# Weights' columns dealt by turns in SBUF, and activations at eight places: one step of a two-layer decoder on Trainium2

## The chip, the cores and the metric

The kernel runs on one core of one Trainium2 chip. The time is device microseconds of one execution. The kernel before took 2747.49 us in the median of three runs (2746.3 to 2748.06). A separate execution was profiled.

The core's engines work from queues of their own: TensorE (matmuls, in the profile PE, and its weight loads, PEld), ScalarE (ACT), VectorE (DVE), GpSimd (POOL) and SyncE (SP, which only issues transfers here).

## The reference

One inference step over 320 tokens, of which 256 are a prompt and 64 are 8 samples of 8 new tokens, with a model width of 2048. Layer 0 mixes tokens by gated linear attention with a carried state, layer 1 by a spatial gate over chunks of 128 positions. Each is followed by a squared-ReLU MLP of width 8192 and each sublayer by a layer norm on the scaled residual:

```python
def sq_relu_mlp(x, w1, w2):
    return jnp.square(jax.nn.relu(x @ w1)) @ w2
...
proj = x @ w_in                                  # gla: q, k, v, r, low-rank gate
...
z = jax.nn.gelu(x @ w_in + b_in, approximate=False)   # spatial gate
...
x = layer_norm(DEEPNORM_ALPHA * x + h, ln1_g[i], ln1_b[i])
x = layer_norm(DEEPNORM_ALPHA * x + sq_relu_mlp(x, mlp_w1[i], mlp_w2[i]), ln2_g[i], ln2_b[i])
```

All inputs are float32. Outputs are the 320 rows, the final states of the attention layer, and the normalised rows of the spatial gate for the samples.

## The kernel before

Activations lie transposed: 128 features on the partitions, 16 k tiles, 320 tokens along the free dimension, so a k tile is 1280 bytes of each partition. Every large product is made of units of weights: 4 k tiles by 256 output features. `unit` (L117) loads one such block of 512 KB with SyncE into `raw` (three buffers), ScalarE casts it to the rounded format `fp32r` as `wh` (L128), and VectorE forms the rest, `wl` = `raw` - `wh` (L129). Activations are split in the same way into a high and a low part, named by the stage: `xh`/`xl` (the layer's input), `oh`/`ol` (attention's output), `yh`/`yl` (the normed input of an MLP or of the spatial gate), `hh`/`hl` (the MLP's inner activations), `ph`/`pl` (the gate's output), `dgh`/`dgl` (a norm's raw input).

`mm3` (L136) issues three matmuls into one PSUM bank for a k tile and one of the two feature tiles `n` of a unit:

```python
nc.tensor.matmul(ps, wl[:, kk, s], x_h, start=first, stop=False)   # L139
nc.tensor.matmul(ps, wh[:, kk, s], x_l, start=False, stop=False)   # L140
nc.tensor.matmul(ps, wh[:, kk, s], x_h, start=False, stop=last)    # L141
```

The stationary operand is 128 x 128 words of weights, the moving operand 128 x 320 words of activations. Each matmul has a weight load of its own. A unit is 2 x 4 x 3 = 24 matmuls, and `group` (L143) runs over four units in the k direction for one or two blocks of 256 columns before the PSUM banks are evicted.

The buffers of `wh` and `wl` are a ring: four of each in ring `a`. When the attention stage is nearly over, its buffers are released (`second_half`, L612) and a second ring `b` of four and four is opened; from then on units take the rings by turns. `bigtile` (L170 and after) allots the activations' tiles with 322 words per k tile; the argument `starts` shifts a view by some words inside its tile. The MLP (L784) runs in four chunks of 2048 inner features: a product with `w1` to `hh`/`hl`, then a product with `w2` that is added to the residual `z`.

The order on each engine is set by the framework's scheduler from the program's dependencies and its own costs; semaphores between engines follow from the tiles. In the attention stage the steps of the recurrence (class `Head`) are laid between units as side work. Three of its tiles matter here: `kend` and `vfm`, which share one tag with two buffers, and the square `sq` in `sample_o` (L571), which has a buffer of its own.

Of the kernel before, what the change touches and what calls it, by code (L numbers as in the profile page):

```python
# [8 lines left out]
F32 = mybir.dt.float32  # L9
F32R = mybir.dt.float32r  # L10
# [5 lines left out]
P = 128  # L16
D = 2048
KT = D // P
TP = 256
DB, DS = 8, 8  # L20
T = TP + DB * DS
TW = T + 2
# [8 lines left out]
UK = 4  # L31
UN = 256
NU = KT // UK


V_BG, V_NG = 0, 8
# [5 lines left out]
class Ring:  # L42


    def __init__(self, pool, tag):
        self.pool, self.tag = pool, tag


class Side:
# [17 lines left out]
def step_kernel(ctx: ExitStack, tc: tile.TileContext, A):  # L67
    nc = tc.nc
    uid = [0]

    def nm(s):
        uid[0] += 1
        return f"{s}_{uid[0]}"


    cp = ctx.enter_context(tc.tile_pool(name="cp", bufs=1))
    big = ctx.enter_context(tc.tile_pool(name="big", bufs=1))
    wraw = ctx.enter_context(tc.tile_pool(name="wraw", bufs=3))
    wa = ctx.enter_context(tc.tile_pool(name="wa", bufs=4))
# [2 lines left out]
    gl = gls.enter_context(tc.tile_pool(name="gl", bufs=4, space=bass.MemoryType.PSUM))  # L82
    mx = None

    rings = [Ring(wa, "a")]
    turn = [0]
    banks = [0]
    units = [0]
# [20 lines left out]
    nc.vector.memset(eps_l[:], LN_EPS)  # L109
    eps_h = cp.tile([P, 1], F32, tag="epsh", name="eps_h")  # L110
    nc.vector.memset(eps_h[:], HEAD_EPS)

    def col(c):
        return vec[:, c : c + 1]


    def unit(w, row0, q, col0, ring):  # L117

        raw = wraw.tile([P, UK, UN], F32, tag="raw", name=nm("raw"))
        src = w[row0 // (UK * P) + q, col0 // UN]  # L120
        hi = ring.pool.tile([P, UK, UN], F32R, tag="h" + ring.tag, name=nm("wh"))
        lo = ring.pool.tile([P, UK, UN], F32R, tag="l" + ring.tag, name=nm("wl"))
        units[0] += 1
        step = 2 if units[0] <= 2 else UK
        for k in range(0, UK, step):
            ks = slice(k, k + step)
            nc.sync.dma_start(raw[:, ks, :], src[:, ks, :])
            nc.scalar.copy(hi[:, ks, :], raw[:, ks, :])  # L128
            nc.vector.tensor_sub(lo[:, ks, :], raw[:, ks, :], hi[:, ks, :].bitcast(F32))  # L129
        return hi, lo  # L130

    def next_ring():
        turn[0] += 1
        return rings[turn[0] % len(rings)]

    def mm3(ps, wh, wl, kk, n, rh, rl, k, c0, cn, first, last):  # L136
        s = slice(n * P, (n + 1) * P)
        x_h, x_l = rh[:, k, c0 : c0 + cn], rl[:, k, c0 : c0 + cn]
        nc.tensor.matmul(ps, wl[:, kk, s], x_h, start=first, stop=False)  # L139
        nc.tensor.matmul(ps, wh[:, kk, s], x_l, start=False, stop=False)  # L140
        nc.tensor.matmul(ps, wh[:, kk, s], x_h, start=False, stop=last)  # L141

    def group(w, row0, cols, rh, rl, evict, side=None, width=T, before=None):  # L143

# [25 lines left out]
    lp = l2 = z = None  # L170
# [4 lines left out]

    def bigtile(tag, dt, name, width=T, start=0):

        t = (lp if tag == "b1" else big).tile([P, KT * TW], dt, tag=tag, name=nm(name))
        return t[:, start : start + KT * width].rearrange("p (k t) -> p k t", t=width)

    def parts(pair, name, width=T, starts=(0, 0)):
        return (bigtile(pair + "0", F32R, name + "h", width, starts[0]),
                bigtile(pair + "1", F32R, name + "l", width, starts[1]))
# [5 lines left out]
    gp = gst.enter_context(tc.tile_pool(name="gp", bufs=1))  # L189
    g2 = gst.enter_context(tc.tile_pool(name="g2", bufs=2))  # L190
# [28 lines left out]
    for c in range(2):  # L219
        m = gp.tile([P, 4, DS], F32, tag=f"ms{c}", name=f"ms{c}")  # L220
# [72 lines left out]
    class Head:  # L293


        def __init__(hd, h):
            hd.h = h
            hd.eb, hd.ei, hd.ee = {}, {}, {}
# [261 lines left out]
        def sample_o(hd):  # L560
            h, s1 = hd.h, hd.s1
            os_ = gp.tile([P, DV], F32, tag="sq", name=nm("os"))
            nc.scalar.copy(os_[:], hd.po[:])
            pt = gltile()
            for vt in range(4):
                nc.tensor.transpose(pt[:, vt * P : (vt + 1) * P], os_[:, vt * P : (vt + 1) * P], ident[:])
            pv = pt[:].rearrange("p (v c t) -> p v c t", v=4, c=2)
            o_s = o_all[:, 4 * h : 4 * h + 4, TP:T]
            nc.scalar.copy(o_s, pv[:, :, 0, :])
            nc.vector.tensor_add(o_s, o_s, pv[:, :, 1, :])  # L570
            sq = gp.tile([P, 4, DB * DS], F32, tag="sqs", name=nm("sq"))  # L571
            nc.scalar.activation(sq[:], o_s, AF.Square)
            nc.vector.tensor_reduce(s1[:, TP:T], sq[:].rearrange("p v t -> p t v"), axis=AX.X, op=ALU.add)

            pr = gltile(T)
            nc.tensor.matmul(pr[:], ones[:], s1[:], start=True, stop=True)
            hd.rs = gp.tile([P, T], F32, tag="rs", name=nm("rs"))
            rsqrt(hd.rs[:], pr[:], 1.0 / DV, HEAD_EPS, eps_h, gp)
# [17 lines left out]
    for h, hd in enumerate(hds):  # L596
        gates = [hd.gate_logits, hd.gate_sums, hd.gate_decays]
        first = [lambda: [load_x(1), load_gates()], lambda: [load_x(q) for q in (2, 3)], low_gate, *gates]
# [13 lines left out]
    def second_half():  # L612

        nonlocal lp, l2, z, gl, mx
        side.flush()
        split_o(range(4 * (H - 1), 4 * H))
        gst.close()
        gls.close()
        gl = ctx.enter_context(tc.tile_pool(name="gs", bufs=2, space=bass.MemoryType.PSUM))
        mx = ctx.enter_context(tc.tile_pool(name="mx", bufs=2, space=bass.MemoryType.PSUM))  # L620
        banks[0] = 3
        lp = ctx.enter_context(tc.tile_pool(name="lp", bufs=1))
        l2 = ctx.enter_context(tc.tile_pool(name="l2", bufs=2))
        wb = ctx.enter_context(tc.tile_pool(name="wb", bufs=4))
        rings.append(Ring(wb, "b"))
        z = lp.tile([P, KT, T], F32, tag="z", name="z")
        for q in range(2):
            nc.gpsimd.dma_start(z[:, 8 * q : 8 * q + 8, :], xT[:, 8 * q : 8 * q + 8, :])
# [122 lines left out]
    def gemm_of(norm, out, w, col0, evict_raw, evict, starts=(0, 0)):  # L751

        yh, yl = parts(out, "y", starts=starts)
        norm.close()
        side = Side([lambda j=j: norm.apply(j, yh, yl) for j in range(KT)], 3 * NU)
        group(w, 0, (col0, col0 + UN), *norm.raw, evict_raw, side, width=TW)
        side.flush()
        for i in range(2, D // UN):
            group(w, 0, (col0 + i * UN,), yh, yl, lambda n, ps, i=i: evict(2 * i + n, ps))
        return yh, yl  # L760
# [23 lines left out]
    def mlp(i, norm, y_in, h_in, vg, vb, raw, last=False):  # L784

        w1, w2 = A["mlp_w1"][i], A["mlp_w2"][i]
        NC_ = 4
        for c in range(NC_):
            hs = []

            def sq_relu(j, x, r):
                if not hs:
                    hs.extend(parts(h_in, "h", starts=(8 * c, 8 * c) if i == 0 else (0, 8 * c)))
                hh, hl = hs
                f = l2.tile([P, T], F32, tag="f", name=nm("f"))
                nc.vector.scalar_tensor_tensor(f[:], x, 0.0, r[:], op0=ALU.max, op1=ALU.mult)
                nc.scalar.copy(hh[:, j, 0:T], f[:])
                nc.vector.tensor_sub(hl[:, j, 0:T], f[:], hh[:, j, 0:T].bitcast(F32))

            def evict(j, ps):  # L800
                r = l2.tile([P, T], F32, tag="r", name=nm("r"))
                nc.scalar.activation(r[:], ps[:], AF.Relu)  # L802
                sq_relu(j, ps[:], r)

            def evict_raw(j, ps):
                t, wb_ = norm.correct(ps)
                r = l2.tile([P, T], F32, tag="r", name=nm("r"))
                nc.scalar.activation(r[:], t[:], AF.Relu, bias=wb_)
                sq_relu(j, r[:], r)

            if c == 0:
                yh, yl = gemm_of(norm, y_in, w1, 0, evict_raw, evict, starts=(0, 0) if i == 0 else (32, 0))
            else:
                gemm(w1, 0, c * D, yh, yl, evict)
            if c < NC_ - 1:
                def evz(j, ps, s=ALPHA if c == 0 else 1.0):
                    nc.vector.scalar_tensor_tensor(z[:, j, :], z[:, j, :], s, ps[:], op0=ALU.mult, op1=ALU.add)
                gemm(w2, c * D, 0, *hs, evz)
            else:
                return residual_gemm(w2, *hs, c * D, 1.0, vg, vb, raw, last=last)  # L820
# [4 lines left out]
    def before(q):  # L825
        if q == NU - 1:
            second_half()

    norm = residual_gemm(A["gla_w_out"], oh, ol, 0, ALPHA, V_L1G, V_L1B, "b", quad=True,
                         side=side, before=before)  # L830
    norm = mlp(0, norm, "a", "b", V_L2G, V_L2B, "a")


# [40 lines left out]
    yh, yl = gemm_of(norm, "b", A["sg_w_in"], D, ev_v_raw, lambda j, ps: put_v(j, ps[:], col(V_SB + KT + j)))  # L874
# [49 lines left out]

    norm = residual_gemm(A["sg_w_out"], ph, pl, 0, ALPHA, V_L1G + KT, V_L1B + KT, "a", quad=True)
    norm = mlp(1, norm, "b", "a", V_L2G + KT, V_L2B + KT, "b", last=True)


    on_pool = (5, 9, 13)
    dh, dl = norm.raw  # L930
    ps = {}
# [98 lines left out]
```

## Time and profile before

| | |
|---|---|
| median of three runs | 2747.49 us |
| the profiled execution | 2747.28 us |
| its span, first to last instruction | 2745.6 us |
| TensorE busy | 2726.5 us in 18,493 matmuls |
| VectorE busy | 1544.6 us |
| ScalarE busy | 1182.2 us |
| mean granted clock of TensorE | 0.999 |
| transfers | 434.51 MB, mean 158 GB/s |

In the profile a line such as L141 is a line of the kernel. A group's row has line, engine, operation, output <- inputs, partitions x elements and count, then busy microseconds and mean nanoseconds of one, then the engine's idle time ahead of these instructions and what ended it. Matmuls are pipelined, so their durations overlap; the distance from start to start tells what one costs. In a view by windows, each engine has its busy time and its number of instructions, and behind them stand the granted clock, the share of the DMA engines and GB/s. A waits row reads: who <- for whom, microseconds in total, times, the longest.

### The profile page before, as it was taken

How to read it: one execution, taken by the hardware profiler on the slowest of the kernel's cores; microseconds unless marked ns; L12 is line 12 of the kernel's file. 1: busy time of each engine (PE TensorE's matmuls, PEld its weight loads, DVE VectorE, ACT ScalarE, POOL GpSimd, SP SyncE). 2: the span in 40 equal slices, each digit the busy share in tenths (PEclk: the TensorE clock that was granted, in tenths of full speed). 3: DMA queues.
4: the chain of work that ended last, by engine and by line, in shares of the span. 5: the costliest groups of instructions: out<-in, count | busy, mean ns of one | idle time of the engine just before them, and what ended most of it. 6: DMA issues, size and time to landing. Idle time of an engine off the chain costs nothing.

```text
span 2745.6 us, 44621 instructions
## 1 busy us (share of the span) xinstructions
PE 2726.5 (99%) x18493; PEld 2703.0 (98%) x18493; DVE 1544.6 (56%) x2284; ACT 1182.2 (43%) x1698; POOL 54.4 (2%) x84
## 2 busy tenths in 40 slices
PE   8999999999999999999999999999999999999998
PEld 8999999999999999999999999999999999999998
DVE  6577577885444434444468774686444444444446
ACT  5545455464334334323345554455334333323433
POOL 1000000000000000000001000000000000000001
PEclk9999999999999999999999999999999999999999
DMA  6557566644444444444445444454444444444442
GB/s 224 178 191 237 163 209 212 208 145 154 152 148 153 147 150 150 152 148 150 150 146 169 148 138 130 141 160 154 147 153 147 153 149 151 149 151 149 151 148 75
DMA packets 126395, 434.51 MB, mean 158 GB/s; under 512 B 13680, under 2 KB 17904, under 8 KB 126192
## 3 DMA queue, kind: packets, MB, share of 16 engines
q1 hardware_dynamic: 118800, 407.29, 47.4%
q0 software_dynamic: 6512, 23.20, 2.4%
q8 instruction: 144, 2.36, 0.4%
q10 hardware_dynamic: 880, 1.18, 0.1%
q14 instruction: 59, 0.48, 0.1%
HBM read 409.60 MB, written 22.02 MB: 157 GB/s over the span
## 4 chain that ended last, share of the span: by engine, by line
PE 98%; DVE 1%; ACT 1%; DMA 0%; issue 0%; SPq 0%; ACTq 0%; DVEq 0%
PE mm L139 31%; PE mm L141 31%; PE mm L140 31%; PE gl L551 1%; PE gl L554 1%; PE gl L509 1%; DMA xr<-xT 0%; PE gl L889 0%; PE gl L493 0%; ACT z L963 0%; PE gl L884 0%; PE gl L494 0%; PE gl L418 0%; PE gl L420 0%; PE gl L472 0%
## 5 line engine op out<-in xcount | busy, mean ns | idle before, releaser
L129 DVE TENSOR_TENSOR wl<-raw,wh 128x1024 fp32r<-128x1024 f32 (+1 forms) x738 | 900.9, 1222 | 966.2 <-ACT wh L128 963.7
L128 ACT CAST wh<-raw 128x1024 fp32r<-128x1024 f32 (+1 forms) x738 | 771.0, 1046 | 1235.4 <-PE mm L141 1120.1
L141 PE MATMUL mm<-yh,wh 128*128 128x320 f32 x2368 | 730.9, 309 | 0.0
L140 PE MATMUL mm<-yl,wh 128*128 128x320 f32 x2368 | 728.5, 308 | 0.0
L139 PE MATMUL mm<-yh,wl 128*128 128x320 f32 x2368 | 725.5, 309 | 0.0
L141 PE MATMUL mm<-hh,wh 128*128 128x320 f32 x2048 | 632.2, 309 | 0.0
L139 PE MATMUL mm<-hh,wl 128*128 128x320 f32 x2048 | 631.8, 309 | 0.0
L140 PE MATMUL mm<-hl,wh 128*128 128x320 f32 x2048 | 631.4, 308 | 0.0
L140 PEld LDWEIGHTS mm<-yl,wh 128*128 128x128 f32 x2368 | 444.8, 188 | 0.0
L141 PEld LDWEIGHTS mm<-yh,wh 128*128 128x128 f32 x2368 | 444.0, 188 | 0.0
L139 PEld LDWEIGHTS mm<-yh,wl 128*128 128x128 f32 x2368 | 443.0, 188 | 0.0
L139 PEld LDWEIGHTS mm<-hh,wl 128*128 128x128 f32 x2048 | 385.0, 188 | 0.0
L140 PEld LDWEIGHTS mm<-hl,wh 128*128 128x128 f32 x2048 | 384.5, 188 | 0.0
L141 PEld LDWEIGHTS mm<-hh,wh 128*128 128x128 f32 x2048 | 384.3, 188 | 0.0
L139 PE MATMUL mm<-xh,wl 128*128 128x320 f32 x768 | 242.1, 316 | 8.7 <-ACT xh L202 5.6
L140 PE MATMUL mm<-xl,wh 128*128 128x320 f32 x768 | 240.8, 314 | 0.0
L141 PE MATMUL mm<-xh,wh 128*128 128x320 f32 x768 | 239.2, 311 | 0.0
L139 PEld LDWEIGHTS mm<-xh,wl 128*128 128x128 f32 x768 | 145.8, 190 | 13.6 <-ACT xh L202 5.6
L140 PEld LDWEIGHTS mm<-xl,wh 128*128 128x128 f32 x768 | 145.8, 190 | 3.5 <-issue 1.2
L141 PEld LDWEIGHTS mm<-xh,wh 128*128 128x128 f32 x768 | 145.9, 190 | 1.3
L139 PE MATMUL mm<-ph,wl 128*128 128x320 f32 x256 | 78.6, 309 | 1.0 <-ACT ph L922 1.0
L802 ACT ACTIVATE r<-mm 128x320 f32<-128x320 f32 x120 | 52.5, 438 | 62.1 <-PE mm L141 62.1
(271 smaller groups left out, 2490.2 us busy)
## 6 DMA issues: line engine op xcount, KB each, us to landing
raw<-mlp_w SPq DMA_DIRECT2D x512, 512.0 KB, 3.5
raw<-gla_w_in SPq DMA_DIRECT2D x94, 512.0 KB, 3.8
raw<-sg_w_in SPq DMA_DIRECT2D x64, 512.0 KB, 3.6
st<-state SPq DMA_DIRECT2D x32, 512.0 KB, 4.2
o_state_s<-st POOLq DMA_DIRECT2D x32, 512.0 KB, 4.1
raw<-gla_w_out SPq DMA_DIRECT2D x32, 512.0 KB, 3.7
raw<-sg_w_out SPq DMA_DIRECT2D x32, 512.0 KB, 3.6
z<-xT POOLq DMA_DIRECT2D x2, 1280.0 KB, 11.3
```

The lines of the kernel that those rows point to most:

```text
L128: nc.scalar.copy(hi[:, ks, :], raw[:, ks, :])
L129: nc.vector.tensor_sub(lo[:, ks, :], raw[:, ks, :], hi[:, ks, :].bitcast(F32))
L139: nc.tensor.matmul(ps, wl[:, kk, s], x_h, start=first, stop=False)
L140: nc.tensor.matmul(ps, wh[:, kk, s], x_l, start=False, stop=False)
L141: nc.tensor.matmul(ps, wh[:, kk, s], x_h, start=False, stop=last)
L509: nc.tensor.matmul(pu[:], hd.ktp[:, blk, kt * P : (kt + 1) * P], hd.vtp[:, blk, :], start=(blk == 0), stop=(blk == 1))
L551: nc.tensor.matmul(po[:], qm[:, kt, b * P : (b + 1) * P], part[:], start=False, stop=(b == DB - 1 and kt == 1 and part is sth))
L554: nc.tensor.matmul(pu[:], kz[:, g, i, kt * P : (kt + 1) * P], hd.vts[:, g, :], start=True, stop=True)
L802: nc.scalar.activation(r[:], ps[:], AF.Relu)
```

## The change

The words of a unit's weights are laid out in another order in SBUF. In ring `a` (`k` = 1) the columns of the two feature tiles take turns: word 2c is column c of the first, word 2c + 1 column c of the second. In ring `b` (`k` = 2) the two feature tiles of two k tiles take turns, four columns in 16 bytes. So a weight load reads 128 words with a step of 8 bytes in ring `a` and of 16 bytes in ring `b`, where it read 512 contiguous bytes. The cast and the subtraction write in that step; `raw` is read as before.

Second, all tiles of activations and weights are set to start at a multiple of 256 bytes or of 128 bytes (small filling tiles see to it; `wl` lies 128 bytes off `wh`). Third, the views of the MLP's activations start at places that differ from chunk to chunk, given by a table: eight places, 32 bytes apart within 256 bytes, one for each of the four chunks in the two layers, where the high and the low part come to lie at the same place. Fourth, `sq` in `sample_o` takes a buffer of the tag that `kend` and `vfm` have.

```diff
+LINE = 64
+BIG = KT * T + LINE
+
+PLACES = [[(0, 32), (16, 48), (32, 0), (48, 16), (0, 32)],
+          [(8, 8), (24, 24), (40, 40), (56, 56), (16, 32)]]
...
-    def __init__(self, pool, tag):
-        self.pool, self.tag = pool, tag
+    def __init__(self, pool, tag, k):
+        self.pool, self.tag, self.k, self.gap = pool, tag, k, False
+
+    def part(self, p, name):
+
+        t = self.pool.tile([P, UK, UN], F32R, tag=p + self.tag, name=name)
+        if not self.gap:
+            self.pool.tile([P, LINE // 2], F32, tag="gap", name=name + "_gap", bufs=1)
+            self.gap = True
+        return t[:].rearrange("p k n -> p (k n)").rearrange("p (a c m) -> p a m c", c=P, m=2 * self.k)
...
-    rings = [Ring(wa, "a")]
+    rings = [Ring(wa, "a", 1)]
...
-        hi = ring.pool.tile([P, UK, UN], F32R, tag="h" + ring.tag, name=nm("wh"))
-        lo = ring.pool.tile([P, UK, UN], F32R, tag="l" + ring.tag, name=nm("wl"))
+        hi = ring.part("h", nm("wh"))
+        lo = ring.part("l", nm("wl"))
...
-            nc.scalar.copy(hi[:, ks, :], raw[:, ks, :])
-            nc.vector.tensor_sub(lo[:, ks, :], raw[:, ks, :], hi[:, ks, :].bitcast(F32))
-        return hi, lo
+            a = slice(k // ring.k, (k + step) // ring.k)
+            r = raw[:, ks, :].rearrange("p (a k) (n c) -> p a (k n) c", k=ring.k, c=P)
+            nc.scalar.copy(hi[:, a], r)
+            nc.vector.tensor_sub(lo[:, a], r, hi[:, a].bitcast(F32))
+        return [lambda kk, n, t=t: t[:, kk // ring.k, 2 * (kk % ring.k) + n] for t in (hi, lo)]
...
-        s = slice(n * P, (n + 1) * P)
         x_h, x_l = rh[:, k, c0 : c0 + cn], rl[:, k, c0 : c0 + cn]
-        nc.tensor.matmul(ps, wl[:, kk, s], x_h, start=first, stop=False)
-        nc.tensor.matmul(ps, wh[:, kk, s], x_l, start=False, stop=False)
-        nc.tensor.matmul(ps, wh[:, kk, s], x_h, start=False, stop=last)
+        nc.tensor.matmul(ps, wl(kk, n), x_h, start=first, stop=False)
+        nc.tensor.matmul(ps, wh(kk, n), x_l, start=False, stop=False)
+        nc.tensor.matmul(ps, wh(kk, n), x_h, start=False, stop=last)
...
-        t = (lp if tag == "b1" else big).tile([P, KT * TW], dt, tag=tag, name=nm(name))
+        t = (lp if tag == "b1" else big).tile([P, BIG], dt, tag=tag, name=nm(name))
...
-            sq = gp.tile([P, 4, DB * DS], F32, tag="sqs", name=nm("sq"))
+            sq = g2.tile([P, 4, DB * DS], F32, tag="vfm", name=nm("sq"))
...
-        rings.append(Ring(wb, "b"))
+        rings.append(Ring(wb, "b", 2))
+        wb.tile([P, 3 * LINE // 4], F32, tag="fill", name="fill_b", bufs=1)
...
-                    hs.extend(parts(h_in, "h", starts=(8 * c, 8 * c) if i == 0 else (0, 8 * c)))
+                    hs.extend(parts(h_in, "h", starts=PLACES[i][c]))
...
-                yh, yl = gemm_of(norm, y_in, w1, 0, evict_raw, evict, starts=(0, 0) if i == 0 else (32, 0))
+                yh, yl = gemm_of(norm, y_in, w1, 0, evict_raw, evict, starts=PLACES[i][-1])
```

The order of instructions stays the same on SyncE and GpSimd, and almost the same on the other engines. In the second half ScalarE's row keeps its order and the casts change their form. The place is the first MLP's norm, where casts stand between the parts of `y`; first the kernel before, then the changed one (a number behind a name is a buffer's).

```order
L729 ACTIVATE z<-t_6066,vec 128x320
L728 ACTIVATE yh_6011<-t_6102,vec 128x320
L729 ACTIVATE z<-t_6102,vec 128x320
L128 CAST wh_6549<-raw_6548 128x1024
L728 ACTIVATE yh_6011<-t_6108,vec 128x320
L729 ACTIVATE z<-t_6108,vec 128x320
L128 CAST wh_6579<-raw_6578 128x1024
```

```order
L745 ACTIVATE z<-t_6070,vec 128x320
L744 ACTIVATE yh_6015<-t_6106,vec 128x320
L745 ACTIVATE z<-t_6106,vec 128x320
L144 CAST wh_6553<-raw_6552 128x2x4x128
L744 ACTIVATE yh_6015<-t_6112,vec 128x320
L745 ACTIVATE z<-t_6112,vec 128x320
L144 CAST wh_6583<-raw_6582 128x4x2x128
```

Ring `b` has the form 2x4x128 (two groups of four columns by turns) and ring `a` 4x2x128; nothing is moved there.

What does move lies in the attention stage, where the square's new buffer sets a new order on VectorE. It is the place where the second head's keys are evicted and the first head is finished, before and after.

```order
L372 TENSOR_TENSOR kend_1675<-kte_1667,fac 128x256
L378 TENSOR_TENSOR kst_1677<-kte_1667,kst_1677 128x8x16
L364 TENSOR_TENSOR kte_1667<-mm_1277,ee_1333 128x320
L570 TENSOR_TENSOR o_all_90<-o_all_90,gl_1576 128x4x64
L365 TENSOR_TENSOR kip_1666<-mm_1277,ei_1318 128x256
L366 TENSOR_TENSOR kis_1668<-mm_1277,ei_1318 128x256
L129 TENSOR_TENSOR wl_1782<-raw_1780,wh_1781 128x1024
L372 TENSOR_TENSOR kend_1693<-kte_1667,fac 128x256
L378 TENSOR_TENSOR kst_1695<-kte_1667,kst_1695 128x8x16
L397 SCALAR_TENSOR_TENSOR qd_1664<-mm_1278,eb_1311 128x320
L573 TENSOR_REDUCE s_132_1012<-sq_1583 128x64
```

```order
L387 TENSOR_TENSOR kend_1677<-kte_1669,fac 128x256
L393 TENSOR_TENSOR kst_1697<-kte_1669,kst_1697 128x8x16
L412 SCALAR_TENSOR_TENSOR qd_1666<-mm_1280,eb_1313 128x320
L588 TENSOR_REDUCE s_132_1014<-sq_1585 128x64
L472 SCALAR_TENSOR_TENSOR o_all_91<-o_all_91,vec,sr_1075 128x320
L472 SCALAR_TENSOR_TENSOR o_all_91<-o_all_91,vec,sr_1077 128x320
L472 SCALAR_TENSOR_TENSOR o_all_91<-o_all_91,vec,sr_1274 128x320
L472 SCALAR_TENSOR_TENSOR o_all_91<-o_all_91,vec,sr_1276 128x320
L412 SCALAR_TENSOR_TENSOR qd_1666<-mm_1281,eb_1319 128x320
L415 TENSOR_TENSOR qx_1667<-qd_1666,fac 128x192
L415 TENSOR_TENSOR qx_1667<-qd_1666,fac 128x128
L387 TENSOR_TENSOR kend_1695<-kte_1669,fac 128x256
```

The first `kend` has moved down to where the second stood, and the second goes behind the reduction of the square, whose buffer it waits for. On TensorE the transposes of `kend` follow, at the same place:

```order
L140 MATMUL mm_1718<-xl_89,wh_1751 128x320
L141 MATMUL mm_1718<-xh_88,wh_1751 128x320
L576 MATMUL gl_1586<-s_132_1012,ones 128x320
L382 MATMUL gl_1680<-ident,kend_1675 128x128 x2
L384 MATMUL gl_1680<-ident,kst_1677 128x128 x2
L382 MATMUL gl_1698<-ident,kend_1693 128x128 x2
L384 MATMUL gl_1698<-ident,kst_1695 128x128 x2
L139 MATMUL mm_1718<-xh_88,wl_1752 128x320
```

```order
L155 MATMUL mm_1720<-xl_90,wh_1753 128x320
L156 MATMUL mm_1720<-xh_89,wh_1753 128x320
L591 MATMUL gl_1588<-s_132_1014,ones 128x320
L397 MATMUL gl_1682<-ident,kend_1677 128x128 x2
L399 MATMUL gl_1682<-ident,kst_1679 128x128 x2
L154 MATMUL mm_1720<-xh_89,wl_1754 128x320
```

The first four transposes stand three matmuls earlier than before, and the other four stand fifteen matmuls behind these.

More of the change, by code (lines that the diff above doesn't have):

```diff
@@ L111, in step_kernel @@
     nc.vector.memset(eps_h[:], HEAD_EPS)
+    cp.tile([P, LINE - 8], F32, tag="fill", name="fill")
     def col(c):
```

## The prediction

> **What bounds the kernel now.** I read the engine table first, then the chain that ended last, then the costliest groups, then the timeline inside one stage.
>
> ```profile
> span 2745.6 us, 44621 instructions
> PE 2726.5 (99%) x18493; PEld 2703.0 (98%) x18493; DVE 1544.6 (56%) x2284; ACT 1182.2 (43%) x1698; POOL 54.4 (2%) x84
> PE 98%; DVE 1%; ACT 1%; DMA 0%; issue 0%; SPq 0%; ACTq 0%; DVEq 0%
> L141 PE MATMUL mm<-yh,wh 128*128 128x320 f32 x2368 | 730.9, 309 | 0.0
> L141 PE MATMUL mm<-hh,wh 128*128 128x320 f32 x2048 | 632.2, 309 | 0.0
> ...
> L139 PE MATMUL mm<-xh,wl 128*128 128x320 f32 x768 | 242.1, 316 | 8.7 <-ACT xh L202 5.6
> ```
>
> TensorE is busy for the whole span and carries 98% of the chain. A row's 309 ns is a pipelined duration; what a matmul costs is the distance between starts. That is read from the timeline, here of the matmuls and of their weight loads in one second-layer gemm, and from a long stretch.
>
> ```profile
> 1000.07 0.31 PE L139 MATMUL mm<-hh,wl 128*128 128x320 f32 x1
> 1000.21 0.32 PE L140 MATMUL mm<-hl,wh 128*128 128x320 f32 x1
> 1000.22 0.19 PEld L141 LDWEIGHTS mm<-hh,wh 128*128 128x128 f32 x1
> 1000.37 0.31 PE L141 MATMUL mm<-hh,wh 128*128 128x320 f32 x1
> 1000.37 0.19 PEld L139 LDWEIGHTS mm<-hh,wl 128*128 128x128 f32 x1
> 1000.51 0.31 PE L139 MATMUL mm<-hh,wl 128*128 128x320 f32 x1
> 700.00:1100.00 400.00, 400.00 (x2729) 400.00 (x2728) 175.79 (x196) 140.21 (x166) 0.00 (x0) 1.00 0.48 150
> ```
>
> The load for the next matmul starts with the running one (1000.22 beside 1000.21). In the stretch 400.00 / 2729 = 0.1466 us per matmul. One window at half the granted clock shows what 320 words cost without disturbance:
>
> ```profile
> 45.80:49.00 3.20, 3.20 (x14) 3.20 (x13) 3.20 (x12) 1.52 (x6) 0.00 (x0) 0.50 0.39 148
> 47.03 0.47 PE L139 MATMUL mm<-xh,wl 128*128 128x320 f32 x1
> 47.30 0.47 PE L140 MATMUL mm<-xl,wh 128*128 128x320 f32 x1
> 47.56 0.47 PE L141 MATMUL mm<-xh,wh 128*128 128x320 f32 x1
> 47.83 0.47 PE L139 MATMUL mm<-xh,wl 128*128 128x320 f32 x1
> ```
>
> There the step is (47.83 - 47.03) / 3 = 0.267 us, so at full clock it should be 0.133. It is 0.1466: 13.3 ns are lost per matmul at full pace and nothing at half pace. So the loss is no fixed switching cost. I read it as the moving stream and the weight stream getting in each other's way in SBUF. This loss, 17,664 x 13.3 ns = 235 us, is what a placement or a stride of the operands can win or multiply.
>
> **The change, part by part.** The number of matmuls, casts and transfers is the same. Of the three matmul lines each has 2368 + 2048 + 768 + 256 + 256 + 192 = 5888 matmuls (y, h, x, o, p, dg), 17,664 together, 736 units of 24. The built order has 317 units in the second ring (four columns by turns) and 419 in the first (two by turns): 7,608 and 10,056 matmuls.
>
> *Weight loads, first ring.* A load reads every second word, two words in each 16 bytes, where it read four. No row shows such a load. Lower end: the two streams no longer cross and the 13.3 ns go, -134 us. Upper end: the loss goes by 16-byte groups touched (32 before, 64 now) and doubles, +134 us. I take 0, the present step, in the middle of the two.
>
> *Weight loads, second ring.* A load reads one word in each 16 bytes. The nearest row for one word per place is on VectorE: a reduction that reads 256 words with a step of 256 bytes, beside a sum of 256 contiguous words and the two sizes of the weights' subtraction.
>
> ```profile
> L573 DVE TENSOR_REDUCE s<-sq x4: 611/615/615, 155.9 to 467.4; 128x64 f32<-128x256 f32 x4
> L499 DVE TENSOR_TENSOR s<-sq x4: 419/424/425, 95.9 to 421.9; 128x256 f32<-128x256 f32 x4
> L129 DVE TENSOR_TENSOR wl<-raw,wh 128x1024 fp32r<-128x1024 f32 x734 | 898.2, 1224 | 963.2 <-ACT wh L128 960.7 <-PE mm L141 0.9
> L129 DVE TENSOR_TENSOR wl<-raw,wh 128x512 fp32r<-128x512 f32 x4 | 2.7, 686 | 3.0 <-ACT wh L128 3.0
> 81.25 1.00 PEld L520 LDWEIGHTS gl<-qd,kis 128*128 128x128 f32 x8
> ```
>
> Contiguous, a word costs (1224 - 686) / 512 = 1.05 ns with 148 ns fixed. The reduction's words cost (614 - 148) / 256 = 1.82 ns, 1.73 times as much. The last row is the pace of loads when their matmuls are only 32 wide: (1.00 - 0.19) / 7 = 0.116 us per load. That is hidden under 0.1466 now; times 1.73 it is 0.201 us and no longer hidden: TensorE would wait for weights. 7,608 x (0.201 - 0.1466) = +414 us. Lower end: no penalty, 0 (and -101 if the 13.3 ns go here too). Upper end: two times 0.116, 7,608 x (0.232 - 0.1466) = +650 us. I take +414, since the reduction is the one row that reads one word per place, though its step is 16 times longer and its engine another.
>
> [...]
>
> *Casts and subtractions.* They now write (VectorE also reads) with a step of 8 or 16 bytes. Lower end nothing; upper end 0.77 ns for each word in the second ring: 1024 x 0.77 = 0.79 us, so the subtraction takes 2.0 us and the cast (1.05 us) 1.84 us. I take 0 on the path. What hides it is a unit's 24 x 0.1466 = 3.5 us on TensorE and the fact that these engines wait for it:
>
> ```profile
> ACT wh L128 <- PE mm L141: 1120.1, 496, 3.8
> DVE wl L129 <- ACT wh L128: 963.7, 571, 3.7
> ```
>
> The casts wait 1120 us for buffers that TensorE frees, so they run ahead by the ring's depth. VectorE would go from 1545 to at most 1545 + 317 x 0.79 = 1795 us. If the cover were gone, one unit would cost its subtraction instead of its matmuls, which at 2.0 against 3.5 us it isn't. At the start two half units lie on the path; 512 x 0.77 ns each would add 0.8 us at most.
>
> *Places of the activations.* Before, the low part's place differs among the second layer's four stages.
>
> ```profile
> 2163.00:2273.00 110.00, 110.00 (x756) 110.00 (x755) 45.76 (x48) 34.01 (x34) 0.00 (x0) 1.00 0.49 153
> 2388.00:2498.00 110.00, 110.00 (x751) 110.00 (x750) 45.24 (x48) 33.70 (x33) 0.00 (x0) 1.00 0.48 152
> ```
>
> 110 / 756 = 0.1455 against 110 / 751 = 0.1465 us: places alone are worth +-0.4%, +-11 us over the span. I take 0.
>
> *The square in the state layer* moves to a buffer that `kend` and `vfm` also use. `kend` of the second key tile goes behind the reduction on VectorE in three heads, and its transposes 12 matmuls later on TensorE, which has other matmuls in between. Behind `kend` on VectorE stand the weights of the next unit, which are loaded ahead. Ends: 0 and 3 x 0.6 us; I take 1 us. SyncE's and GpSimd's rows keep their order, and alignment alone issues nothing.
>
> **Sum.** The profiled execution took 2747.28 us (span 2745.6), 0.2 below the median of the three runs, 2747.49. 2747.3 + 0 + 414 + 0 + 0 + 1 = 3162, called 3160.
>
> **Rivals.**
> 1. *Both streams keep step (faster).* At full pace 320 words of 4 bytes move in 0.133 us, 9.6 bytes/ns. Loads at 0.116 us per 128 words move 4.4 bytes/ns contiguous and 8.8 with the new step of 8 bytes, nearly the moving stream's pace. If the loss comes from one stream passing the other, it goes in the first ring: 2747 - 134 = 2613, or 2512 if the second ring gains as well. For it: nothing is lost at half pace, and the loss depends on places. Against: the places moved it by 0.4% only. It decides as long as the second ring's step stays below 0.1466 + 134 / 7608 = 0.164 us.
> 2. *Loss by 16-byte groups.* 13.3 ns for 32 groups; 64 and 128 groups give 0.160 and 0.187 us: 2747 + 134 + 7,608 x 0.040 = 3185. For it: the step is close to the same everywhere. Against: no row with another number of groups.
> 3. *A small penalty in the second ring only*, such as one more 13.3 ns: 2747 + 101 = 2848.
> 4. *Nothing happens:* loads stay hidden and the loss stays, 2747 +-11. For it: a load takes 0.19 us in every row whatever runs beside it. Against: the half-clock window, which shows that something gives way.
>
> [...]
>
> **How the numbers follow.** The forecast (first ring as now, second ring bound by its loads) has 0.40, the loss by groups 0.15, the small penalty 0.12, the gain 0.27, nothing 0.06. Slower by over 0.2%, about what can be told from no change here, is 0.40 + 0.15 + 0.12 = 0.67; faster 0.27; same 0.06. The range for 8 in 10 runs from 2613, the first gain, rounded to 2610, to 3330, between the forecast and its upper end of 3397; outside are the double gain and the upper tail. The forecast's own range is 3030 (with the first ring's gain) to 3330.
>
> **What would show it.** Right: in the second half of the span the starts of matmuls alternate by unit, 24 near 0.147 and 24 near 0.20 us, with loads longer than 0.19 us, while the first 440 us keep 0.1466. Group law: steps of 0.160 in the first 440 us already. Gain: steps near 0.134 there. The cover of casts: waits for `wh` by TensorE stay near nothing. The forecast is wrong if loads with one word per 16 bytes keep 0.19 us and their pace.

## The result, and the profile after

The changed kernel took 3424.64 us in the median (3424.27 to 3426.16), the kernel before on the same chip 2747.77 us. The ratio is 1.2465 with a 95% interval of 1.2444 to 1.2487: it is slower by a quarter. 3160 us was forecast, and the measured time lies above the range's upper end of 3330.

The profiled execution of the changed kernel took 3426.16 us. Its page first, the engine table and the groups that answer to those shown of before (the changed kernel's lines are 15 further down: L154 to L156 are the three matmuls, L144 the cast, L145 the subtraction):

```profile
span 3424.4 us, 44623 instructions
PE 3400.8 (99%) x18493; PEld 3377.3 (99%) x18493; DVE 1781.2 (52%) x2284; ACT 1517.0 (44%) x1698; POOL 55.1 (2%) x84
PE 98%; DVE 1%; ACT 0%; DMA 0%; issue 0%; SPq 0%; ACTq 0%; DVEq 0%
L145 DVE TENSOR_TENSOR wl<-raw,wh 128x1024 fp32r<-128x1024 f32 (+1 forms) x738 | 1161.7, 1575 | 1449.5 <-ACT wh L144 1445.7
L144 ACT CAST wh<-raw 128x1024 fp32r<-128x1024 f32 (+1 forms) x738 | 1128.3, 1530 | 1520.4 <-PE mm L156 1419.8
L156 PE MATMUL mm<-hh,wh 128*128 128x320 f32 x2048 | 725.3, 354 | 0.0
L156 PEld LDWEIGHTS mm<-hh,wh 128*128 128x128 f32 x2048 | 539.7, 264 | 0.0
```

TensorE still carries 98% of the chain, and it has the same 18,493 matmuls; a duration of L156 on `hh` is 354 ns on the mean, where it was 309. The load's 264 ns are a mean over two rings, which hides both. The timeline at a change of ring shows them apart: matmuls first, then the loads (start, duration).

```profile
1052.53 0.31 PE L155 MATMUL mm<-hl,wh 128*128 128x320 f32 x1
...
1053.26 0.39 PE L154 MATMUL mm<-hh,wl 128*128 128x320 f32 x1
1053.49 0.39 PE L155 MATMUL mm<-hl,wh 128*128 128x320 f32 x1
...
1054.20 0.40 PE L155 MATMUL mm<-hl,wh 128*128 128x320 f32 x1
1052.97 0.20 PEld L156 LDWEIGHTS mm<-hh,wh 128*128 128x128 f32 x1
...
1053.33 0.33 PEld L155 LDWEIGHTS mm<-hl,wh 128*128 128x128 f32 x1
1053.56 0.33 PEld L156 LDWEIGHTS mm<-hh,wh 128*128 128x128 f32 x1
```

Up to 1053.26 the steps are those of the first ring, (1053.26 - 1052.53) / 5 = 0.146 us; from there on of the second, (1054.20 - 1053.26) / 4 = 0.235 us, and a load takes 0.33 instead of 0.20 us. Over the 317 units of the second ring the mean of their median steps is 0.2352 us. That alone is 7,608 x (0.2352 - 0.1466) = +674 us of the 679 us between the profiled executions.

The first 440 us, where only the first ring exists, stayed as they were: the same window before and after (busy time and count of TensorE come first).

```profile
20.00:440.00 420.00, 417.87 (x2763) 398.48 (x2762) 276.47 (x497) 223.19 (x368) 23.24 (x32) 1.00 0.60 196
```

```profile
20.00:440.00 420.00, 417.70 (x2770) 398.28 (x2769) 277.49 (x498) 231.39 (x369) 23.29 (x32) 1.00 0.60 196
```

2763 matmuls before, 2770 after. And TensorE hardly waits for the slower casts and subtractions, 2.6 us in all; the waits after, with who waits for whom, total, times and the longest:

```profile
ACT wh L144 <- PE mm L156: 1419.8, 514, 4.5
DVE wl L145 <- ACT wh L144: 1445.7, 536, 5.4
PE mm L154 <- DVE wl L145: 2.6, 2, 1.6
```

### The profile page after: what moved, and what is told of

Same layout as the page of the kernel before. It is cut to its first block, busy times and chain, and to the rows that moved or that the text cites. A ratio compares the mean times of both kernels' runs of the same rounds, so it can differ in the third digit from the quotient of the medians.

```text
span 3424.4 us, 44623 instructions
## 1 busy us (share of the span) xinstructions
PE 3400.8 (99%) x18493; PEld 3377.3 (99%) x18493; DVE 1781.2 (52%) x2284; ACT 1517.0 (44%) x1698; POOL 55.1 (2%) x84
## 4 chain that ended last, share of the span: by engine, by line
PE 98%; DVE 1%; ACT 0%; DMA 0%; issue 0%; SPq 0%; ACTq 0%; DVEq 0%
PE mm L155 32%; PE mm L154 32%; PE mm L156 31%; PE gl L566 1%; PE gl L569 0%; PE gl L524 0%; PE gl L905 0%; DMA xr<-xT 0%; PE gl L508 0%; DVE wl L145 0%; DMA raw<-gla_w_in 0%; ACT z L979 0%; PE gl L900 0%; ACT wh L144 0%; PE gl L509 0%
## 5 line engine op out<-in xcount | busy, mean ns | idle before, releaser
L145 DVE TENSOR_TENSOR wl<-raw,wh 128x1024 fp32r<-128x1024 f32 (+1 forms) x738 | 1161.7, 1575 | 1449.5 <-ACT wh L144 1445.7
L144 ACT CAST wh<-raw 128x1024 fp32r<-128x1024 f32 (+1 forms) x738 | 1128.3, 1530 | 1520.4 <-PE mm L156 1419.8
L155 PE MATMUL mm<-yl,wh 128*128 128x320 f32 x2368 | 837.7, 354 | 0.3 <-DVE yl L747 0.3
L156 PE MATMUL mm<-yh,wh 128*128 128x320 f32 x2368 | 836.2, 353 | 0.0
L154 PE MATMUL mm<-yh,wl 128*128 128x320 f32 x2368 | 832.1, 354 | 0.0
L156 PE MATMUL mm<-hh,wh 128*128 128x320 f32 x2048 | 725.3, 354 | 0.0
L154 PE MATMUL mm<-hh,wl 128*128 128x320 f32 x2048 | 725.1, 354 | 0.0
L156 PEld LDWEIGHTS mm<-yh,wh 128*128 128x128 f32 x2368 | 622.6, 263 | 0.0
L155 PEld LDWEIGHTS mm<-yl,wh 128*128 128x128 f32 x2368 | 622.0, 263 | 0.5 <-DVE yl L747 0.5
L154 PEld LDWEIGHTS mm<-yh,wl 128*128 128x128 f32 x2368 | 621.3, 263 | 0.0
L155 PEld LDWEIGHTS mm<-hl,wh 128*128 128x128 f32 x2048 | 539.9, 264 | 0.0
L156 PEld LDWEIGHTS mm<-hh,wh 128*128 128x128 f32 x2048 | 539.7, 264 | 0.0
L154 PEld LDWEIGHTS mm<-hh,wl 128*128 128x128 f32 x2048 | 538.8, 263 | 0.0
L154 PE MATMUL mm<-xh,wl 128*128 128x320 f32 x768 | 243.1, 317 | 10.6 <-ACT xh L217 5.7
L156 PE MATMUL mm<-xh,wh 128*128 128x320 f32 x768 | 238.2, 310 | 0.0
L154 PEld LDWEIGHTS mm<-xh,wl 128*128 128x128 f32 x768 | 149.7, 195 | 15.3 <-ACT xh L217 5.7
L156 PEld LDWEIGHTS mm<-xh,wh 128*128 128x128 f32 x768 | 149.9, 195 | 1.2
L154 PE MATMUL mm<-ph,wl 128*128 128x320 f32 x256 | 90.1, 354 | 1.0 <-ACT ph L938 1.0
```

The lines of the kernel that those rows point to most:

```text
L144: nc.scalar.copy(hi[:, a], r)
L145: nc.vector.tensor_sub(lo[:, a], r, hi[:, a].bitcast(F32))
L154: nc.tensor.matmul(ps, wl(kk, n), x_h, start=first, stop=False)
L155: nc.tensor.matmul(ps, wh(kk, n), x_l, start=False, stop=False)
L156: nc.tensor.matmul(ps, wh(kk, n), x_h, start=False, stop=last)
```

## The experiments

The theories on record were: theory 1, a load that reads one word in each 16 bytes is itself slow and sets the step; theory 2, the strided writes of the casts and subtractions hold the path; theory 3, the strided loads slow the moving stream.

**The step of the loads, changed ring by ring.** First the second ring at the first ring's layout, then the first ring at the second's, then a step of 32 bytes in the second.

```diff
-        rings.append(Ring(wb, "b", 2))
+        rings.append(Ring(wb, "b", 1))
```

> The second ring too has its columns by turns of two feature tiles (8-byte step) instead of four; all else as in the changed kernel. Theory 1 (a weight load that reads one word in each 16 bytes is itself slow and sets the step, 0.235 us): the second ring's step falls to the first's 0.147 us and the loss of 677 us goes; time 2747 +-15 us. Theory 2 (the casts' and subtractions' strided writes hold the path): these still write with a step of 8 bytes in both rings; a part of the loss stays, between 2850 and 3100 us. Theory 3 (the strided loads slow the moving stream): as theory 1, if the first ring's step is its measure.

Measured 2752.42 us, 1.0018 of the kernel before (1.0009 to 1.0028). The loss is the second ring's 16-byte step; 8-byte steps in both rings cost 0.2%. The stretch that the prediction showed of before, with 2729 matmuls, has 2745 here, with both rings at work:

```profile
700.00:1100.00 400.00, 400.00 (x2745) 400.00 (x2745) 177.72 (x199) 150.72 (x170) 0.00 (x0) 1.00 0.48 151
```

```diff
-    rings = [Ring(wa, "a", 1)]
+    rings = [Ring(wa, "a", 2)]
```

> Both rings have the columns by turns of four (16-byte step). Theory 1 and 3: every one of the 17,664 matmuls takes 0.235 us: 17,664 x 0.2352 + 158 us of other work = 4313 us. Theory 2: the casts of all 736 units are then of the slower form, 2.0 us each against 24 x 0.235 = 5.6 us of TensorE, and nothing is bound by them; if they disturb by their writes, the step becomes larger than 0.235.

Measured 4303 us in a single run, 10 us from the 4313 expected. Its casts and subtractions (all but the four of half size at the start) are of the second form:

```profile
L144 ACT CAST wh<-raw 128x1024 fp32r<-128x1024 f32 x734 | 1509.2, 2058 | 1892.5 <-PE mm L156 1785.8 <-issue 83.4 <-DMA raw<-gla_w_out 14.1
L145 DVE TENSOR_TENSOR wl<-raw,wh 128x1024 fp32r<-128x1024 f32 x734 | 1496.1, 2039 | 1799.0 <-ACT wh L144 1792.6 <-ACT scst L539 4.3 <-ACT dgh L665 2.0
```

They take 2.06 and 2.04 us, where 1.05 and 1.22 us were needed for contiguous words, and TensorE's 5.6 us per unit hide them. The casts of before, for two sizes, which are needed further down:

```profile
L128 ACT CAST wh<-raw 128x1024 fp32r<-128x1024 f32 x734 | 768.7, 1048 | 1234.8 <-PE mm L141 1120.1 <-issue 38.2 <-DMA raw<-gla_w_out 24.0
L128 ACT CAST wh<-raw 128x512 fp32r<-128x512 f32 x4 | 2.4, 618 | 0.6 <-DMA raw<-gla_w_in 0.5
```

```diff
-        rings.append(Ring(wb, "b", 2))
+        rings.append(Ring(wb, "b", 4))
```

> The second ring has the columns by turns of eight (32-byte step), the first stays at two. Theory 1a (what costs is that each word lies in a 16-byte group of its own, so a longer step costs no more): step stays 0.235 us, time 3424 +-30 us. Theory 1b (the cost grows with the bytes passed over): each doubling of the step adds what the last added, 0.235 + 0.088 = 0.323 us or more, time 4090 us or more.

Measured 3485 us in a single run, 61 us more than with 16 bytes: outside the 30 us that theory 1a allowed, and far from the 4090 of theory 1b. A unit of the second ring in its timeline:

```profile
1502.02 0.40 PE L154 MATMUL mm<-yh,wl 128*128 128x320 f32 x1
...
1506.86 0.40 PE L156 MATMUL mm<-yh,wh 128*128 128x320 f32 x1
```

Twenty steps in 4.84 us are 0.242 us each. Twice the step in bytes adds 3%, where from 8 to 16 bytes the step rose by 60%. So what is paid for here, in the main, is that each word lies in 16 bytes of its own (theory 1a), with a small rest for the longer step: with two words in 16 bytes the load stays hidden (but for 0.2% of the time), with one it sets the step at 0.235 us, and with one in 32 bytes at 0.242 us.

**Writes against reads.** A second view of the same buffers (`part` now returns both, by columns and contiguous) lets the casts write in one layout while the loads read in the other.

```diff
+        his, los = ring.part("h", nm("wh")), ring.part("l", nm("wl"))
+        hi, lo = his[1], los[1]
...
+        return [lambda kk, n, t=t: t[:, kk // ring.k, 2 * (kk % ring.k) + n] for t in (his[0], los[0])]
```

> The cast and the subtraction write contiguous blocks of 128 columns as in the kernel before, but the loads still read with steps of 8 and 16 bytes, so the weights that TensorE multiplies by are the wrong ones and the output is not the reference's. Theory 1 and 3: nothing changes on TensorE, 3424 +-15 us, while VectorE's busy time falls from 1781 to near 1545 us. Theory 2: the loss goes, 2747 +-15 us.

Measured 3420.7 us in a single run. VectorE and ScalarE are back at the load they had before, and the loss stays, all but some 4 us: theory 2 falls.

```profile
PE 3398.9 (99%) x18493; PEld 3375.8 (99%) x18493; DVE 1549.8 (45%) x2284; ACT 1183.0 (35%) x1698; POOL 54.5 (2%) x84
```

The counterpart has the two indices exchanged:

> The counterpart of the run with contiguous casts: the cast and the subtraction write with steps of 8 and 16 bytes as in the changed kernel, and the loads read contiguous blocks (so TensorE multiplies by columns in the wrong order; the output is not the reference's). Theory 1 (only the loads' step costs): 2747 +-11 us, with VectorE still busy some 1780 us. Theory 2 (the strided writes cost as well, in disturbing TensorE's reads): above 2760 us.

Measured 2768.6 us in a single run: the 677 us are gone, but it lies above the 2760 us that were to tell whether the writes cost anything. Against the kernel with contiguous weights and the same places (2746.9 us, below) it is 21.7 us longer. Its span, its engines, three of its waits and one stretch of 3.41 us, then span, engines and two waits of the other:

```profile
span 2766.9 us, 44623 instructions
PE 2732.5 (99%) x18493; PEld 2706.7 (98%) x18493; DVE 1775.5 (64%) x2284; ACT 1508.4 (55%) x1698; POOL 55.2 (2%) x84
```

```profile
PE mm L157 <- DVE yl L749: 8.3, 4, 3.8
PE mm L156 <- DVE wl L147: 8.3, 3, 6.0
PE gl L723 <- DVE a L721: 2.7, 1, 2.7
1517.97:1521.38 3.41, 3.41 (x15) 3.41 (x14) 3.41 (x9) 1.31 (x3) 0.00 (x0) 0.50 0.28 83
```

```profile
span 2743.4 us, 44623 instructions
PE 2723.4 (99%) x18493; PEld 2699.5 (98%) x18493; DVE 1544.2 (56%) x2284; ACT 1182.7 (43%) x1698; POOL 54.8 (2%) x84
```

```profile
PE mm L154 <- ACT xh L217: 5.8, 1, 5.8
PE mm L154 <- DVE wl L145: 1.3, 2, 0.9
```

TensorE stands still for 34.4 instead of 20.0 us and is busy for 9 us more. The longest wait, 6.0 us for `wl`, is that of the first matmul, and the other run has it too (5.8 us for `xh`). New are above all three waits of 2 to 4 us for `yl`, at 610, 1517 and 1878 us, and one of 2.7 us for `a`, all for VectorE. Close behind each of the three for `yl` stands a stretch of 3.41 us at granted clock 0.50, with 13 to 15 matmuls where the clock of 1.00 has 25. There are five such stretches ahead of the end, and none in the other run; five times some ten matmuls of 0.147 us fewer are about 7.5 of the 9 us. So in this single run the slow writes are hidden to all but 0.8% when TensorE has its quick pace; at the slow one they are hidden to all but 4 us.

**The load or the moving stream.** The matmuls of both rings were cut to 32 moving columns, but for the first and last feature tile:

```diff
+        m = 32 if 0 < k < KT - 1 else cn
+        nc.tensor.matmul(ps[:, 0:m], wl(kk, n), x_h[:, 0:m], start=first, stop=False)
```

> The weight matmuls of all but the first and last of the 16 feature tiles move 32 columns instead of 320 (the sums over the other columns leave out these tiles; the output is not the reference's), so that almost nothing moves beside the loads. Steps between matmuls inside a unit are what is to be read. Theory 1 (the load itself is slow): the second ring's step stays between 0.20 and 0.235 us, the first ring's falls to about 0.116. Theory 3 (the strided load slows the moving stream): both rings fall to about 0.116 us. The time of the whole is then also bound by the transfers of the weights and says little.

The whole took 4147 us in a single run, and the granted clock, which the expectation left out, fell to 0.524 on the mean; that the transfers bound this time as well is not shown (the casts waited 1972.4 us in all for TensorE). The steps still tell what was asked. First a unit of the first ring at full clock, then two units at half clock, the second ring's up to 1505.78 and the first ring's after it.

```profile
125.81 0.27 PE L155 MATMUL mm<-xh,wl 128*128 128x32 f32 x1
...
126.40 0.27 PE L157 MATMUL mm<-xh,wh 128*128 128x32 f32 x1
...
1504.84 0.39 PE L157 MATMUL mm<-yh,wh 128*128 128x32 f32 x1
1505.07 0.40 PE L155 MATMUL mm<-yh,wl 128*128 128x32 f32 x1
...
1505.78 0.37 PE L155 MATMUL mm<-yh,wl 128*128 128x32 f32 x1
...
1507.06 0.37 PE L155 MATMUL mm<-yh,wl 128*128 128x32 f32 x1
```

In its windows the granted clock is the third number from the end:

```profile
126.00:127.00 1.00, 1.00 (x9) 1.00 (x9) 1.00 (x2) 0.40 (x1) 0.64 (x1) 1.00 0.61 106
1507.00:1510.00 3.00, 3.00 (x16) 3.00 (x16) 1.96 (x1) 1.01 (x1) 0.00 (x0) 0.50 0.02 5
```

The first ring's step is (126.40 - 125.81) / 5 = 0.118 us at clock 1.00 and (1507.06 - 1505.78) / 6 = 0.213 us at clock 0.50; the second ring's is (1505.78 - 1504.84) / 4 = 0.235 us at half clock too. So the step of the load with a word in 16 bytes is 0.235 us with 32 columns at clock 0.50, as it is with 320 columns at clock 1.00 in the changed kernel. What this run lacks is the second ring at full clock, so two more cut that ring alone, to 160 and to 32 columns (`rk` is the `k` of the unit's ring):

```diff
+        m = 160 if rk == 2 and 0 < k < KT - 1 else cn
```

> Only in the second ring the matmuls of all but the first and last of the 16 feature tiles move 160 columns instead of 320 (the sums over the other columns leave these tiles out; the output is not the reference's). Theory 1 (the load's own price): the second ring's step stays at 0.235 us and the time at 3424 +-15 us. Theory 3 (the moving stream has a part in it): half of the 0.088 us that the step is above the first ring's goes, 0.191 us, and the time falls by up to 7,608 x 0.044 x 14/16 = 293 us to 3131 us.

> The same with 32 columns. Theory 1: the second ring's step stays at 0.235 us, 3424 +-15 us if the granted clock stays full; if it falls to half, the first ring's steps grow to 0.267 us and the second ring's stay. Theory 3: the second ring's step falls below 0.16 us.

Measured 3754 and 3969 us in a single run each; both times were missed, because the clock fell again (0.859 and 0.794 on the mean) and slowed the first ring. The steps are again the answer. In the run with 160 columns, the clock returns within the first ring's unit (steps of 0.267, then 0.148 us), and the second ring's next unit runs at full clock:

```profile
1503.01 0.47 PE L155 MATMUL mm<-hh,wl 128*128 128x320 f32 x1
...
1503.81 0.47 PE L155 MATMUL mm<-hh,wl 128*128 128x320 f32 x1
...
1505.02 0.31 PE L155 MATMUL mm<-hh,wl 128*128 128x320 f32 x1
...
1506.65 0.31 PE L157 MATMUL mm<-hh,wh 128*128 128x320 f32 x1
...
1507.66 0.40 PE L156 MATMUL mm<-hl,wh 128*128 128x160 f32 x1
...
1509.30 0.40 PE L157 MATMUL mm<-hh,wh 128*128 128x160 f32 x1
1507.66:1509.30 1.64, 1.64 (x9) 1.64 (x9) 1.15 (x1) 0.46 (x1) 0.00 (x0) 1.00 0.81 262
```

(1509.30 - 1507.66) / 7 = 0.234 us with half the moving words, at clock 1.00 by the last row. Of the second ring's units with narrow matmuls, 22 with 160 columns and 31 with 32 lie wholly in stretches at clock 1.00, and each of them has a median step of 0.234 or 0.235 us. Theory 3, by which these had to fall to 0.191 and below 0.16 us, is refuted.

**Places.** Contiguous weights with the changed kernel's places:

```diff
-        return t[:].rearrange("p k n -> p (k n)").rearrange("p (a c m) -> p a m c", c=P, m=2 * self.k)
+        return t[:].rearrange("p k n -> p (k n)").rearrange("p (a m c) -> p a m c", c=P, m=2 * self.k)
```

> Contiguous blocks of 128 columns in both rings as in the kernel before, with the changed kernel's places of activations and weights, its fillers and its square. Places cost nothing on the mean: 2747 +-11 us. If places follow the first ring's rows of the changed kernel (144.5 ns at (0,0), 145.8 where one part is at 0 and two of three matmuls read it, 148 elsewhere): some 147.2 on the mean, 2747 + 17,664 x 0.0006 = 2758 us.

Measured 2746.88 us, 0.9998 (0.9989 to 1.0006): the change's places are worth nothing on the mean. They do differ among themselves: for the eight stages of the inner activations the mean step goes from 144.5 ns (both parts at 0) over 145.6 (64 and 192 bytes) to 147.8 ns (32 bytes). Then the best of them for all:

```diff
-PLACES = [[(0, 32), (16, 48), (32, 0), (48, 16), (0, 32)],
-          [(8, 8), (24, 24), (40, 40), (56, 56), (16, 32)]]
+PLACES = [[(0, 0)] * 5] * 2
```

> As the kernel with contiguous weights, and every activation, high and low part, begins at a multiple of 256 bytes. If a matmul whose 1280 moving bytes fill five 256-byte blocks, instead of parts of six, takes 144.5 instead of 148 ns whatever the weights' order: 2747 - 17,664 x 0.0021 = 2710 us. If the 144.5 ns need the columns by turns: 2747 +-11 us.

> Columns by turns of two (8-byte step) in both rings, and every activation at a multiple of 256 bytes. By the rows at (0,0) in the changed kernel every step is 144.5 ns: 2747 - 17,664 x 0.0021 = 2710 us, 1.3% below the kernel before. If the places were only a chance of those stages: 2752 us, as with both rings at two.

Measured 2738.58 us (ratio 0.9968, 0.9956 to 0.9980) and 2728.93 us (0.9934, 0.9921 to 0.9946), both above the 2710 expected: the low parts in the second pair of buffers begin 128 bytes off, so their place was not 0 after all. In the MLP's stages with a low part at 128 bytes the step is 147.8 ns with contiguous weights and 145.6 ns with columns by turns of two, against 144.4 or 144.5 ns in those with both parts at 0. With that put right:

```diff
+        start = (start + (LINE // 2 if tag == "b1" else 0)) % LINE
```

> Contiguous weights, high part at 0 and low part at 128 bytes of 256, and every activation, the low parts in the second pair of buffers too, at a multiple of 256 bytes. The kernel with contiguous weights and first places took 2738.6 us and had 270 units of 24 matmuls with a low part at 128 bytes, at 147.6 instead of 144.5 ns: 2738.6 - 270 x 24 x 0.0031 = 2718 us. If the place is no cause of its own, 2738 us.

> The same places with the columns by turns of two in both rings. By the rows of the kernel with its first places (2728.9 us, 300 units with a low part at 128 bytes at 145.56 instead of 144.45 ns): 2728.9 - 300 x 24 x 0.0011 = 2721 us. If the columns by turns of two are of use by themselves, below the kernel with contiguous weights and the same places; if not, the two agree within 5 us.

> As the kernel with contiguous weights and all activations at multiples of 256 bytes, with the low parts of the weights too at a multiple of 256 bytes instead of 128 bytes behind one. If the place of a load counts as that of the moving rows does, one of three loads touches two 256-byte blocks instead of three, and the step falls by about 1 ns: 2718 - 17.7 = 2700 us; if not, 2718 +-5 us.

Measured 2716.11 us (0.9885, 0.9870 to 0.9900), 2722.48 us (0.9908, 0.9895 to 0.9922) and, with contiguous weights whose low parts are moved by 128 bytes, 2749.55 us (1.0007, 0.9998 to 1.0015). The first is 1.15% faster than the kernel before, the best of all. The first two came near the 2718 and 2721 expected. The last gives it all back. The same 400 us in the first and the last:

```profile
700.00:1100.00 400.00, 400.00 (x2771) 400.00 (x2771) 180.30 (x202) 143.38 (x171) 0.00 (x0) 1.00 0.49 152
```

```profile
700.00:1100.00 400.00, 400.00 (x2729) 400.00 (x2728) 176.55 (x196) 139.74 (x166) 0.00 (x0) 1.00 0.48 149
```

400 / 2771 = 144.4 ns against 400 / 2729 = 146.6 ns, which is the step of the kernel before. So the place counts, but of weights and activations together: it was expected that the weights' low parts at 256 bytes would help by 1 ns, and they cost 2.2. Columns by turns of two bring nothing of their own: at the same places they are 6 us slower (2722.5 against 2716.1 us, where 5 us were allowed for), and with the change's places 5 us (2752.4 against 2746.9). Of these three pairs, only with the low parts at 128 bytes were they faster, by 10 us (2728.9 against 2738.6). What rule ties the places to the step stays open.

## Why the prediction was wrong in its size

- **What bounds the kernel**: right. TensorE's pace is the whole time, before and after.
- **"Weight loads, first ring", taken at 0**: right to 0.2%. 2770 against 2763 matmuls in the window, and +0.18% with both rings in that layout. Its ends of -134 and +134 us, the streams no longer crossing and the loss by 16-byte groups, were both wide of it. That the 13.3 ns are the two streams in each other's way was an estimate, which no run shows; nor does one show the 0.133 us at full clock that they are counted from, for the shortest mean step read here is 144.4 ns.
- **"Weight loads, second ring", taken at +414 us: the step that failed.** The mechanism was right, loads that TensorE has to wait for; the size was 0.235 instead of 0.201 us, +674 us. The prediction took a fitting row, the reduction that reads one word per place, and the wrong thing from it: the ratio to contiguous words, 1.73, applied to the load's 0.116 us. Its price per word would have done. (614 - 148) / 256 = 1.82 ns a word, by 128 words, is 0.233 us. The measured step is 0.2352 / 128 = 1.84 ns, the subtraction in this layout, (2039 - 148) / 1024 = 1.85 ns, and the cast, (2058 - 188) / 1024 = 1.83 ns, with the 188 ns from its 1048 and 618 ns for 1024 and 512 contiguous words. That these four agree so well was seen only afterwards, and why they do is not shown. The ratio did not carry over because the contiguous prices differ: 0.116 us is 0.91 ns a word, against VectorE's 1.05. In the run with 32 columns the load with two words in 16 bytes, 0.118 us at full clock, changes with TensorE's clock (0.213 us at 0.50), which the price of one word in 16 bytes does not (0.235 and 0.234 us at 0.50 and 1.00).
- **The range** was cut at 3330, below the upper end of 3397 that the prediction had worked out from two times 0.116. That end missed by 28 us, of which the step's 3.2 ns over 0.232 are 24. An upper end that has a mechanism was left out to keep the range within 8 in 10.
- **"Casts and subtractions", 0 on the path**: right at this pace (3420.7 us without the slow writes, 4 us less, in a single run). Their size was right for VectorE (2.0 us, at most 1795 us busy; 2.04 and 1781) and low for ScalarE (1.84; 2.06), to whose 1.05 us VectorE's extra 0.77 ns a word had been added. At the quick pace the cover is not whole: about 22 us, in a single run.
- **"Places of the activations", 0 and +-11 us**: right for the places of this change (2746.88 us against 2746.96 for the kernel before beside it). The bounds came from stages whose places are mixed; the places of all operands together were worth 32 us.
- **"The square in the state layer", +1 us**: too small to be told; the changed square is in the kernel with contiguous weights too, which is level with the kernel before.
- **Rivals.** The gain (1) and the loss by groups (2) fall with the first 440 us, where the step stayed, and the loss by groups also with 0.235 us where it had 0.187. The small penalty (3) falls with the size. Nothing (4) falls too: the second ring's step is 0.235 us beside 320, 160 and 32 moving columns alike, so in these runs the load sets the pace without the moving stream holding it up, by taking longer than the 0.147 us of the matmul. Nor was the load's 0.19 us the same whatever ran beside it: in the window at half clock before, 45.80 to 49.00 us, the loads take 0.33 us.

## What to carry to other kernels

Compare a weight load's own price with its matmul's: here it was hidden at 0.118 beside 0.147 us and set the step at 0.235. Read what a strided operand costs as nanoseconds per word from a row with that access, and not as a ratio to another engine's best; here the price per word of VectorE, ScalarE and the weight load agreed within 2%. Keep two words or more in each 16 bytes that a load reads: the step was 0.146 us with two and 0.235 with one. The places of weights and activations together were worth 32 us here, and all of it went when the weights' low parts alone were moved by 128 bytes: try them together, and look at the starts of every tile in the built program, not only at the numbers that are added to them.

## What was not expected of the hardware

- One price of 1.8 to 1.9 ns per word in 16 bytes of its own fits a weight load (0.235 us for 128), VectorE's subtraction (1.85 ns), its reduction with a step of 256 bytes (1.82 ns) and ScalarE's cast (1.83 ns). For the load it is the same at clock 1.00 and 0.50, where the 8-byte load goes from 0.118 to 0.213 us.
- With few moving columns the granted clock fell, though by the profile TensorE was busy for 99% of the span or more: to 0.524 with 32 columns in both rings, 0.794 in the second alone, 0.859 with 160 columns there. Why stays open. The changed kernel itself, whose second ring waits for loads beside 320 columns, kept 0.999.
- 144.4 against 146.6 ns per matmul for 128 bytes in the place of the weights' low parts alone, 33 us over the span. In most of the MLP's stages whose operands all lie at multiples of 64 bytes, with contiguous weights, the mean steps were 144.4 or 144.5, 145.6, 146.7 and 147.8 ns, values some 1.1 ns apart.
